# The up-projection's recombination moved into PSUM banks, and the convolution with it, in a decoder layer on one core

## The chip, the core and the metric

The kernel runs on one core of a Trainium2 chip. TensorE multiplies matrices: it loads a 128x128 weight tile and streams up to 512 columns past it into a bank of PSUM (eight banks of 128 partitions x 512 float32 values). VectorE (DVE in the profile) and ScalarE (ACT) read and write PSUM and the on-chip memory SBUF; GpSimd (POOL) works on SBUF alone; SyncE (SP) issues most DMAs. Each engine works through its own list of instructions in order, and they wait for each other by semaphores. The metric is the device time of one execution in microseconds.

## The reference

One layer on 1024 tokens of 1024 channels, all float32: norm, two kinds of attention with gates, residual, then the part that the change concerns:

```python
def conv_ffn(xn, w_up, conv_w, conv_b, w_down):
    S = xn.shape[1]
    u = xn @ w_up
    upad = jnp.pad(u, ((0, 0), (CONV_WIDTH - 1, 0), (0, 0)))
    c = conv_b
    for j in range(CONV_WIDTH):
        c = c + upad[:, j:j + S] * conv_w[j]
    gate, val = jnp.split(c, 2, axis=-1)
    return (jax.nn.silu(gate) * val) @ w_down
```

Before it stands `rmsnorm(x, norm_ffn_w)`, after it a residual addition and a final norm.

## The kernel before

Everything is kept with channels on partitions and tokens along the row. To keep float32 accuracy each matrix product is made of three matmuls: high half of the weights with high and low half of the activations, low half of the weights with the high half (`product`, lines 828 to 837; a product over 512 input channels into one bank of 128 output channels x 512 tokens is 4 x 3 = 12 matmuls).

The up-projection (`hidden`, lines 839 to 914) runs over 22 pairs j. A pair is 128 gate channels and the 128 value channels that belong to them. Over the two blocks of output channels, the two halves of the input channels and the two halves of the tokens it is a 2 x 2 x 2 product of blocks, and is computed with the seven products of Strassen's method in Winograd's form instead of eight. The weights' blocks are A11, A12 (gate) and A22 (value), and sums S1 to S4 that GpSimd makes (`sum_pair`, lines 86 to 100); ScalarE rounds each to its high half and VectorE subtracts to get the low half (`split_pair`, lines 102 to 115, with the tiles wh and wl for A11/A12 and for A22, two of each, and sh and sl for the sums, three of each). `next_w` keeps this two pairs ahead in the program's order. The activations' blocks B11, B21, B22 and the sums T1 to T4 are made once before.

The seven products P1 = A11 B11, P2 = A12 B21, P5 = S1 T1, P6 = S2 T2, P7 = S3 T3, P3 = S4 B22, P4 = A22 T4 each take a bank of the pool `psF`, eight banks in turn. `recombine` (lines 389 to 402) puts them together: ScalarE copies P1 to SBUF, and VectorE makes seven additions of 512 columns, each of a bank and an SBUF tile, through u2 = P1 + P6, u3 = u2 + P7 and u4 = u2 + P5:

- c11 = P1 + P2 (gate, first tokens), c12 = u4 + P3 (gate, last tokens),
- c21 = u3 - P4 (value, first tokens), c22 = u3 + P5 (value, last tokens).

`glu` (950 to 960) and `conv` (962 to 973) then do, for gate and value, on 1024 columns in SBUF: multiplication by the norm's factor `rstd` (GpSimd, L965; for gate and value of pair 0 VectorE), bias and last tap (ScalarE, L970), two taps (VectorE, L971 and L972); then ScalarE's silu of the gate (L957), VectorE's product of both (L958), and a store of the pair's result to DRAM by SyncE (L959). For the first pair `rstd` itself is spread over the partitions by TensorE's transposes between products.

The order on each engine is set by a planner: of what is ready by its own estimate, it takes what the program issues first. The value convolution of pair 20 and both of pair 21 are put off into the down-projection (`defer`), which begins on the same banks under another pool (`psD`) once they are free.

Of the kernel before, what the change touches and what calls it, by code (L numbers as in the profile page):

```python
# [12 lines left out]
AF = mybir.ActivationFunctionType  # L13
# [4 lines left out]
P = 128  # L18
D = 1024
T = 1024  # L20
# [22 lines left out]
class Trunk:  # L43
# [206 lines left out]
    def project(self):  # L250
# [6 lines left out]
        with ExitStack() as ctx:  # L257
# [22 lines left out]
            def diffs(k):  # L280
# [6 lines left out]
                tt(b, b2, b, ALU.subtract)  # L287
# [101 lines left out]
    def recombine(self, ps, us, tp, o):  # L389
# [12 lines left out]
        tt(c21, u3, ps["P4"], ALU.subtract)  # L402
# [400 lines left out]
    def operands(self, xt, xtp, xw, k):  # L803
# [22 lines left out]
        tt(t4, t2, b21, ALU.subtract)  # L826
# [12 lines left out]
    def hidden(self, pair):  # L839
        nc, tc = self.nc, self.tc  # L840
        with ExitStack() as ctx:
            e = ctx.enter_context
            psF = e(tc.tile_pool(name="psF", bufs=8, space=PSUM, reuse_waits="tile"))
            self.psT = psF
# [6 lines left out]
            ready = {}  # L851
            for j in range(NF):
                w, ps = ready.pop(j) if j else (w0, {})
                if j == 0:
# [9 lines left out]
                    ssq = self.tl(psF, [P, H2], "t")  # L864
# [14 lines left out]
                for name, a, b in (prods[i] for i in ((0, 1, 2, 5, 3, 6, 4) if j == NF - 1 else (0, 1, 2, 5, 3, 4, 6) if j else range(7))):  # L879
                    if name not in ps:  # L880
                        ps[name] = self.tl(psF, [P, H2], "t")
                        self.product(ps[name], w[a], b)
                us = [self.tl(tp, [P, T + 2], "us", bufs=3) for _ in range(2)]
                if j == NF - 1:
                    self.defer.pop(0)(lo)
                    self.xctx2.close()
                    self.uw = None
                    self.open_down()
                    self.deep = True
                    with tc.high_priority(100):  # L890
                        self.ahead(2)
                self.recombine(ps, us, tp, 2)
                if j < NF - 1:
# [6 lines left out]
                    for name, a, b in prods[:2 if j == 0 else 0]:  # L900
                        ps[name] = self.tl(psF, [P, H2], "t")
                        self.product(ps[name], w[a], b)
                if j == 0:
                    for hf in range(2):
                        sp = self.tl(psF, [P, H2], "t")
                        self.spread(sp, rs, hf * 4)
                        nc.scalar.copy(self.rstd[:, hf * H2:(hf + 1) * H2], sp)

                for w in range(2):
                    f = lambda after=None, j=j, w=w, us=us: self.glu(j, w, us[w], tp, after)  # L910
                    if j + w < NF - 1:
                        f()
                    else:
                        self.defer.append(f)
# [296 lines left out]
```

## Time and profile before

| | |
|---|---|
| median of 3 runs | 1356.72 us (1356.71 to 1357.4) |
| the profiled execution | 1356.2 us, span of its instructions 1354.3 us |
| granted TensorE clock, mean | 0.996 |
| the up-projection's products | from about 684 us to 1111 us of the span |

In a timeline, each row is: start in us, duration in us, engine, line, operation, output tile <- input tiles, shape, count, and in brackets the idle time before it and what ended it. Tile names come from the program; every bank of `psF` is called t. In a table of windows, each row is: window, its length, then busy time and instruction count of TensorE, its weight loads, VectorE, ScalarE and GpSimd, granted clock, share of the DMA engines, GB/s. In a list of groups: line, engine, operation, tiles, shape, count, busy us, mean ns of one, idle us before them and what ended it. In a list of waits: who waited for whom, us in total, times, longest. `L837 t<-B_0h,wl` is a product's third matmul on its first block of input channels.

### The profile page before, as it was taken

Reading aid. Unit: us, or ns where it says so; the run is one execution under the profiler, and the core shown is the slowest. Engines: PE = TensorE matmul, PEld = TensorE weight load, DVE = VectorE, ACT = ScalarE, POOL = GpSimd, SP = SyncE. Lnnn points to the kernel's source line nnn. Section 1 sums busy time; section 2 is a strip of 40 time slices with the busy share of each in tenths; the row PEclk is TensorE's granted clock in tenths of the full one; section 3 lists DMA queues with packets and bytes.
Section 4 is the critical chain, followed back from the end, with each engine's and each line's share of the span. In section 5 each row is a group of like instructions: output and inputs, shape, how many; then the busy total and the mean of one; then the engine's idle time right before and its main releaser. Section 6 shows DMA issues by size and latency. Waiting matters only on the chain.

```text
span 1354.3 us, 17160 instructions
## 1 busy us (share of the span) xinstructions
PE 1335.0 (99%) x6304; PEld 1103.6 (81%) x6304; DVE 1009.8 (75%) x1454; ACT 603.9 (45%) x942; POOL 483.1 (36%) x350
## 2 busy tenths in 40 slices
PE   7999999999999999999999999999999999999997
PEld 6888888888887777878888888888888888888886
DVE  8846775388898875355689888888888898986454
ACT  8422232376667664334444334433443345433343
POOL 0436651010102125741455565555555611231011
PEclk9999999999999999999999999999999999999999
DMA  6334443966554235334422222122212248651342
GB/s 255 140 113 164 143 156 114 272 174 175 156 133 144 77 116 219 117 119 136 166 82 88 71 91 94 62 79 93 93 63 83 92 141 311 215 177 64 94 134 85
DMA packets 62470, 179.50 MB, mean 133 GB/s; under 512 B 6833, under 2 KB 15153, under 8 KB 62385
## 3 DMA queue, kind: packets, MB, share of 16 engines
q1 hardware_dynamic: 50928, 160.98, 36.7%
q10 hardware_dynamic: 11456, 17.41, 3.5%
q8 instruction: 50, 0.82, 0.2%
q14 instruction: 36, 0.29, 0.1%
HBM read 129.61 MB, written 48.76 MB: 132 GB/s over the span
## 4 chain that ended last, share of the span: by engine, by line
PE 62%; DVE 17%; POOL 7%; issue 7%; DMA 4%; ACT 3%; POOLq 0%; DVEq 0%; SPq 0%; ACTq 0%
PE t L836 7%; PE t L837 7%; PE t L835 7%; POOL us L965 3%; PE y L996 3%; PE d L996 3%; PE sc L568 3%; PE g L150 2%; PE g L151 2%; DVE c L958 2%; PE g L152 2%; DVE wl L112 2%; DMA gr<-gd 2%; PE sc L151 2%; PE sc L152 2%
## 5 line engine op out<-in xcount | busy, mean ns | idle before, releaser
L970 ACT ACTIVATE c<-us,vecs 128x1024 f32<-128x1024 f32 x44 | 54.8, 1248 | 163.2 <-POOL us L965 160.0
L965 POOL TENSOR_TENSOR us<-us,rstd 128x1024 f32<-128x1024 f32 x42 | 100.7, 2414 | 52.8 <-DVE wl L131 34.3
L110 ACT CAST sh<-sf 128x1024 fp32r<-128x1024 f32 x62 | 64.9, 1051 | 106.2 <-POOL sf L97 61.8
L129 ACT CAST wh<-raw 128x1024 fp32r<-128x1024 f32 (+2 forms) x60 | 60.7, 1012 | 104.8 <-PE sc L151 33.1
L971 DVE SCALAR_TENSOR_TENSOR c<-us,vecs,c 128x1024 f32<-128x1024 f32 x44 | 67.1, 1527 | 51.9 <-ACT c L970 51.9
L131 DVE TENSOR_TENSOR wl<-raw,wh 128x1024 fp32r<-128x1024 f32 (+2 forms) x60 | 75.3, 1256 | 39.1 <-ACT wh L129 29.3
L96 POOL TENSOR_TENSOR sf<-rv 128x512 f32<-128x512 f32 x30 | 42.5, 1417 | 166.7 <-DMA rv<-in_w_up 73.2
L112 DVE TENSOR_TENSOR sl<-sf,sh 128x1024 fp32r<-128x1024 f32 x62 | 88.3, 1426 | 8.2 <-ACT sh L110 8.2
L167 POOL TENSOR_TENSOR rs<-ms,mhalf 128x8 f32<-128x8 f32 (+2 forms) x9 | 14.5, 1614 | 159.1 <-DVE ms L165 148.5
L150 PE MATMUL g<-xh,wh 128*128 128x512 f32 x176 | 70.7, 402 | 0.1
L152 PE MATMUL g<-xh,wl 128*128 128x512 f32 x176 | 70.4, 400 | 0.0
L151 PE MATMUL g<-xl,wh 128*128 128x512 f32 x176 | 70.4, 400 | 0.0
L98 POOL TENSOR_TENSOR sf<-raw,rv 128x512 f32<-128x512 f32 x30 | 41.6, 1386 | 59.9 <-DVE sl L112 59.9
L572 DVE CUSTOM_DVE_ANT_0 L<-sc,bias 128x128 f32<-128x128 f32 (+7 forms) x64 | 47.7, 752 | 17.4 <-PE sc L568 14.1
L551 POOL MEMSET aT<- 128x128 f32 x32 | 6.1, 204 | 152.0 <-PE t L597 101.6
L573 ACT ACTIVATE L<-L,sm 128x128 f32<-128x128 f32 (+7 forms) x64 | 49.6, 778 | 20.7 <-DVE sm L572 18.2
L97 POOL TENSOR_TENSOR sf<-sf,raw 128x512 f32<-128x512 f32 x31 | 58.0, 1870 | 1.6
L972 DVE SCALAR_TENSOR_TENSOR c<-us,vecs,c 128x1024 f32<-128x1024 f32 x44 | 56.2, 1279 | 0.6
L725 POOL TENSOR_TENSOR gr<-gr,rstd 128x1024 f32<-128x1024 f32 x16 | 39.4, 2467 | 41.4 <-DMA gr<-gd 41.2
L112 DVE TENSOR_TENSOR wl<-raw,wh 128x1024 fp32r<-128x1024 f32 (+1 forms) x35 | 52.8, 1508 | 0.1
L151 PE MATMUL sc<-ml,wh 128*128 128x512 f32 x128 | 50.1, 391 | 0.6 <-DVE ml L746 0.6
L568 PE MATMUL sc<-u,u 128*128 128x512 f32 (+2 forms) x192 | 49.8, 359 | 0.1
(444 smaller groups left out, 4351.4 us busy)
## 6 DMA issues: line engine op xcount, KB each, us to landing
u<-qd SPq DMA_DIRECT2D x72, 256.0 KB, 6.1
raw<-in_w_down SPq DMA_DIRECT2D x27, 512.0 KB, 3.7
raw<-in_w_in SPq DMA_DIRECT2D x25, 512.0 KB, 4.4
hr<-hd SPq DMA_DIRECT2D x50, 256.0 KB, 5.3
raw<-in_w_up SPq DMA_DIRECT2D x23, 512.0 KB, 3.6
hd<-c SPq DMA_DIRECT2D x22, 512.0 KB, 2.8
rv<-in_w_up SPq DMA_DIRECT2D x21, 512.0 KB, 3.5
gr<-gd SPq DMA_DIRECT2D x16, 512.0 KB, 3.6
```

The costliest lines, as they stand in the source:

```text
L112: nc.vector.tensor_tensor(lo, src, hi.bitcast(F32), ALU.subtract)
L131: self.lo = (eng or nc.vector).tensor_tensor(wl, raw, wh.bitcast(F32), ALU.subtract)
L150: nc.tensor.matmul(ps, wh[:, kc + o, :], ah, start=first and n == 0, stop=False)
L151: nc.tensor.matmul(ps, wh[:, kc + o, :], al, start=False, stop=False)
L152: nc.tensor.matmul(ps, wl[:, kc + o, :], ah, start=False, stop=last and n == len(kcs) - 1)
L568: nc.tensor.matmul(sc[:, lo + n0:lo + n1], qs, k[c][part][:, n0:n1], start=part == 0, stop=part == 1)
L835: nc.tensor.matmul(ps, ah[:, k, :], bh, start=first and n == 0, stop=False, skip_group_check=skip)
L836: nc.tensor.matmul(ps, ah[:, k, :], bl, start=False, stop=False, skip_group_check=skip)
L837: nc.tensor.matmul(ps, al[:, k, :], bh, start=False, stop=last and n == len(ks) - 1, skip_group_check=skip)
L965: i = (nc.vector if m % NF == 0 else nc.gpsimd).tensor_tensor(us[:, 2:], us[:, 2:], self.rstd, ALU.mult)
L971: nc.vector.scalar_tensor_tensor(c, us[:, 1:T + 1], cw[1], c, ALU.mult, ALU.add)
L996: nc.tensor.matmul(ps, v[:, n, :], x, start=n == i == 0, stop=n == len(js) - 1 and i == 2)
```

## The change

From the second pair on (j >= 1), the seven products go through four banks a, b, c, d instead of seven, and most sums are made by letting further matmuls add to what a bank holds:

- a = A11 B11 (`begin`); ScalarE copies a to b. Then b gets S2 T2 added, which makes u2; ScalarE copies b to c. d = S1 T1, copied by ScalarE to an SBUF tile s5.
- a gets A12 B21 added: c11. c gets S3 T3 added: u3. b gets S4 B22 added.
- VectorE empties a with one multiplication by `rstd` (`scaled`); out of c it adds s5 to make c22, out of b it adds s5 to make c12 (`summed`), and GpSimd multiplies these two halves by `rstd`.
- c then gets A22 T4 added and is emptied by `scaled`: c21. T4 has its sign turned where it is made, here and in the first projection, so that it can be added.
- The order of products is a pair's A11, the previous pair's A22 (`last`, issued by the next pair through `rest`), then S2, S1, A12, S3, S4. In pair 1 S1's product stands ahead, before the norm's transposes; in the last pair A22 follows S4 directly.

The convolution from pair 1 on is made in halves of 512 columns in two banks, psC: ScalarE's first tap writes the bank, VectorE's two taps work in it, ScalarE's silu or VectorE's product takes it out to SBUF. One of the two banks has a tag of its own (s). The value convolution of a pair is issued in the next pair, after A22's product. The convolutions of pair 21, in the down-projection, stay in SBUF at full width, without the multiplication by `rstd`, which is done before.

```diff
@@ -284,7 +284,7 @@
-                tt(b, b2, b, ALU.subtract)
+                tt(b, b, b2, ALU.subtract)
@@ -399,7 +399,7 @@
-        tt(c21, u3, ps["P4"], ALU.subtract)
+        tt(c21, ps["P4"], u3, ALU.add)
@@ -823,7 +823,7 @@
-        tt(t4, t2, b21, ALU.subtract)
+        tt(t4, b21, t2, ALU.subtract)
@@ -840,15 +840,15 @@
         nc, tc = self.nc, self.tc
         with ExitStack() as ctx:
             e = ctx.enter_context
-            psF = e(tc.tile_pool(name="psF", bufs=8, space=PSUM, reuse_waits="tile"))
-            self.psT = psF
+            psF = self.psT = e(tc.tile_pool(name="psF", bufs=7, space=PSUM, reuse_waits="tile"))
+            self.psC = None
             xc2 = e(tc.tile_pool(name="xc2", bufs=1, side="right", reuse_waits="tile"))
             self.uw = e(tc.tile_pool(name="uw", bufs=3, side="right", reuse_waits="tile"))
             prods = (("P1", "A11", "B11"), ("P2", "A12", "B21"), ("P5", "S1", "T1"), ("P7", "S3", "T3"),
                      ("P3", "S4", "B22"), ("P6", "S2", "T2"), ("P4", "A22", "T4"))
             with tc.high_priority(400):
                 w0 = self.split_pair(*pair)
-            ready = {}
+            ready, rest = {}, None
             for j in range(NF):
                 w, ps = ready.pop(j) if j else (w0, {})
                 if j == 0:
@@ -861,7 +861,7 @@
                         self.B["T4", k], self.B["T2", k] = ((hi[:, c], lo[:, c]) for c in (slice(0, H2), slice(H2, T)))
                     self.tctx.close()
                     tp = e(tc.tile_pool(name="tp", bufs=2, side="right", reuse_waits="tile"))
-                    ssq = self.tl(psF, [P, H2], "t")
+                    ssq = self.tl(psF, [P, H2], "s", bufs=1)
                     for n, (name, a, b) in enumerate(prods[:5]):
                         self.product(ps[name], w[a], b, (3,), first=False)
                         if n == 4:
@@ -876,20 +876,25 @@
                                 h = self.tl(self.uw, [P, 2, H2], ("sh", "sl", "rv", "rv", "sh", "sl")[2 * k + hf], F32R, **({"bufs": 2} if k == 1 else {}))
                                 self.hs[hf, k] = self.split(h[:, 0], h[:, 1], r[:, hf * H2:(hf + 1) * H2])
                         lo = self.lo
-                for name, a, b in (prods[i] for i in ((0, 1, 2, 5, 3, 6, 4) if j == NF - 1 else (0, 1, 2, 5, 3, 4, 6) if j else range(7))):
-                    if name not in ps:
-                        ps[name] = self.tl(psF, [P, H2], "t")
-                        self.product(ps[name], w[a], b)
-                us = [self.tl(tp, [P, T + 2], "us", bufs=3) for _ in range(2)]
-                if j == NF - 1:
-                    self.defer.pop(0)(lo)
-                    self.xctx2.close()
-                    self.uw = None
-                    self.open_down()
-                    self.deep = True
-                    with tc.high_priority(100):
-                        self.ahead(2)
-                self.recombine(ps, us, tp, 2)
+                if j == 0:
+                    for name, a, b in prods:
+                        if name not in ps:
+                            ps[name] = self.tl(psF, [P, H2], "t")
+                            self.product(ps[name], w[a], b)
+                    us = [self.tl(tp, [P, T + 2], "us", bufs=3) for _ in range(2)]
+                    self.recombine(ps, us, tp, 2)
+                else:
+                    us, last = self.chain(w, ps or self.begin(psF, w), tp, rest)
+                    rest = last
+                    if j == NF - 1:
+                        self.defer.pop(0)(lo)
+                        self.xctx2.close()
+                        self.uw = None
+                        self.open_down()
+                        self.deep = True
+                        with tc.high_priority(100):
+                            self.ahead(2)
+                        rest()
                 if j < NF - 1:
 
                     w, ps = ready[j + 1] = self.next_w(), {}
@@ -897,21 +902,76 @@
                         raw = [self.tl(self.sfp[0], [P, T], "t42", bufs=1)] + [self.tl(self.sfp[0], [P, T], "sf") for _ in range(2)]
                         for k, r in enumerate(raw):
                             nc.sync.dma_start(r, self.hd[k])
-                    for name, a, b in prods[:2 if j == 0 else 0]:
-                        ps[name] = self.tl(psF, [P, H2], "t")
-                        self.product(ps[name], w[a], b)
                 if j == 0:
+                    ps.update(self.begin(psF, w))
+                    self.product(ps["d"], w["S1"], "T1")
                     for hf in range(2):
-                        sp = self.tl(psF, [P, H2], "t")
+                        sp = self.tl(psF, [P, H2], "s", bufs=1)
                         self.spread(sp, rs, hf * 4)
                         nc.scalar.copy(self.rstd[:, hf * H2:(hf + 1) * H2], sp)
 
-                for w in range(2):
-                    f = lambda after=None, j=j, w=w, us=us: self.glu(j, w, us[w], tp, after)
-                    if j + w < NF - 1:
-                        f()
+                if j:
+                    self.psC = [self.tl(psF, [P, H2], "s", bufs=1), self.tl(psF, [P, H2], "t")]
+                first, second = (lambda after=None, j=j, w=w, us=us: self.glu(j, w, us[w], after, j > 0) for w in range(2))
+                if j == NF - 1:
+                    self.defer += [first, second]
+                else:
+                    first()
+                    if j == NF - 2:
+                        self.defer.append(second)
+                    elif j == 0:
+                        second()
                     else:
-                        self.defer.append(f)
+                        rest = lambda last=last, second=second: (last(), second())
+
+    def begin(self, pool, w):
+
+        ps = {n: self.tl(pool, [P, H2], "t") for n in "adbc"}
+        self.product(ps["a"], w["A11"], "B11", skip=True)
+        self.nc.scalar.copy(ps["b"], ps["a"])
+        return ps
+
+    def chain(self, w, ps, tp, rest):
+
+        nc = self.nc
+        tt = nc.vector.tensor_tensor
+        a, b, c, d = (ps[n] for n in "abcd")
+        us = [None, None]
+
+        def half(r, hf):
+            if us[r] is None:
+                us[r] = self.tl(tp, [P, T + 2], "us", bufs=3)
+            return us[r][:, 2 + hf * H2:2 + hf * H2 + H2], self.rstd[:, hf * H2:(hf + 1) * H2]
+
+        def scaled(r, hf, p):
+            u, rs = half(r, hf)
+            tt(u, p, rs, ALU.mult)
+
+        def summed(r, hf, p):
+            u, rs = half(r, hf)
+            tt(u, p, s5, ALU.add)
+            nc.gpsimd.tensor_tensor(u, u, rs, ALU.mult)
+
+        if rest:
+            rest()
+        self.product(b, w["S2"], "T2", first=False, skip=True)
+        nc.scalar.copy(c, b)
+        if rest:
+            self.product(d, w["S1"], "T1")
+        s5 = self.tl(tp, [P, H2], "s1", bufs=1)
+        nc.scalar.copy(s5, d)
+        self.product(a, w["A12"], "B21", first=False, skip=True)
+        scaled(0, 0, a)
+        self.product(c, w["S3"], "T3", first=False, skip=True)
+        summed(1, 1, c)
+        self.product(b, w["S4"], "B22", first=False, skip=True)
+        summed(0, 1, b)
+
+        def last():
+            self.product(c, w["A22"], "T4", first=False, skip=True)
+            scaled(1, 0, c)
+
+        return us, last
 
     def open_down(self):
         tc = self.tc
@@ -947,30 +1007,39 @@
         tt(b21, b22, b21, ALU.subtract)
         self.B["T4", k] = self.parts_h(b21)
 
-    def glu(self, j, w, us, tp, after):
-
-        nc = self.nc
-        c = self.conv(j + w * NF, us, tp, after)
+    def glu(self, j, w, us, after, scaled):
+
+        nc = self.nc
         if w == 0:
-            self.c0 = c
+            self.c0 = self.tl(self.cpl, [P, T], "c")
+        for c, a, b in self.conv(j + w * NF, us, after, scaled):
+            g = self.c0[:, a:b]
+            if w == 0:
+                nc.scalar.activation(g, c, AF.Silu)
+            else:
+                nc.vector.tensor_tensor(g, g, c, ALU.mult)
+        if w == 0:
             return
-        nc.scalar.activation(self.c0, self.c0, AF.Silu)
-        nc.vector.tensor_tensor(self.c0, self.c0, c, ALU.mult)
         store = lambda c0=self.c0: nc.sync.dma_start(self.hd[j], c0)
         self.late.append(store) if after is not None else store()
 
-    def conv(self, m, us, tp, after=None):
+    def conv(self, m, us, after, scaled):
         nc = self.nc
         nc.gpsimd.memset(us[:, 0:2], 0.0)
-        i = (nc.vector if m % NF == 0 else nc.gpsimd).tensor_tensor(us[:, 2:], us[:, 2:], self.rstd, ALU.mult)
-        if after is not None:
-            self.tc.add_manual_dep(i.ins, after.ins.name, mybir.DependencyInfo(mybir.DependencyClass.Sync, mybir.DependencyReason.DATA), reason="later")
-        c = self.tl(self.cpl, [P, T], "c")
+        if not scaled:
+            (nc.vector if m % NF == 0 else nc.gpsimd).tensor_tensor(us[:, 2:], us[:, 2:], self.rstd, ALU.mult)
         cw = [self.vecs[:, C_CW + 3 * m + k:C_CW + 3 * m + k + 1] for k in range(3)]
-        nc.scalar.activation(c, us[:, 2:], AF.Identity, bias=self.vecs[:, C_CB + m:C_CB + m + 1], scale=cw[2])
-        nc.vector.scalar_tensor_tensor(c, us[:, 1:T + 1], cw[1], c, ALU.mult, ALU.add)
-        nc.vector.scalar_tensor_tensor(c, us[:, 0:T], cw[0], c, ALU.mult, ALU.add)
-        return c
+        for a, b in ((0, H2), (H2, T)) if self.psC else ((0, T),):
+            if self.psC:
+                c = self.psC[a // H2]
+            else:
+                c = self.c0 if m < NF else self.tl(self.cpl, [P, T], "c")
+            i = nc.scalar.activation(c, us[:, 2 + a:2 + b], AF.Identity, bias=self.vecs[:, C_CB + m:C_CB + m + 1], scale=cw[2])
+            if after is not None:
+                self.tc.add_manual_dep(i.ins, after.ins.name, mybir.DependencyInfo(mybir.DependencyClass.Sync, mybir.DependencyReason.DATA), reason="later")
+            nc.vector.scalar_tensor_tensor(c, us[:, 1 + a:1 + b], cw[1], c, ALU.mult, ALU.add)
+            nc.vector.scalar_tensor_tensor(c, us[:, a:b], cw[0], c, ALU.mult, ALU.add)
+            yield c, a, b
 
     def down(self):
 
@@ -982,6 +1051,7 @@
             self.uw = e(tc.tile_pool(name="uwd", bufs=2, side="right", reuse_waits="tile"))
             self.hpb = e(tc.tile_pool(name="hpb", bufs=HPB, side="right", reuse_waits="tile"))
             self.sfp = self.cpl, "c"
+            self.psC = None
             self.B = {}
             tt = nc.vector.tensor_tensor
             bank = lambda n: self.tl(psD, [P, H2], "dy"[n])
```

## The prediction

> **What bounds the kernel now.** I read the page's busy table and its chain first, then the up-projection in stretches, then who waited for whom, then one period of each engine's timeline.
>
> ```profile
> span 1354.3 us, 17160 instructions
> PE 1335.0 (99%) x6304; PEld 1103.6 (81%) x6304; DVE 1009.8 (75%) x1454; ACT 603.9 (45%) x942; POOL 483.1 (36%) x350
> ```
>
> TensorE is nearly always busy, so only holes in its stream can be won. Windows of the up-projection (us, then busy time and instructions of each engine):
>
> ```profile
> 706.26:726.22 19.96, 19.96 (x94) 16.60 (x92) 19.67 (x19) 10.79 (x12) 12.20 (x9) 1.00 0.26 80
> 726.22:821.42 95.20, 95.20 (x422) 78.85 (x420) 81.07 (x79) 36.46 (x39) 53.83 (x40) 1.00 0.25 83
> 821.42:1072.61 251.19, 250.94 (x1093) 204.05 (x1092) 215.45 (x209) 97.22 (x104) 141.82 (x105) 1.00 0.25 82
> 1072.61:1111.07 38.46, 38.38 (x169) 31.45 (x168) 34.76 (x40) 14.85 (x19) 13.35 (x11) 1.00 0.29 92
> ```
>
> A pair is 7 products of 12 matmuls, 84 weight loads. The second row is 420 of them, five pairs (2 to 6): 95.20/420 = 0.2267 us each, 2.72 us a product, 19.04 a pair, and nothing is lost. The third is 13 pairs: 251.19 against 1092 x 0.2267 = 247.5, so 3.65 us lost. The fourth is the last two: 38.46 against 38.08, 0.38 lost. **All that the up-projection after its first pair can give back is 4.0 us, 0.30% of the run.** What is lost, and to whom:
>
> ```profile
> PEld t L837 <- DVE wl L112: 5.7, 14, 0.5
> ACT c L970 <- POOL us L965: 152.9, 39, 8.8
> DVE c L971 <- ACT c L970: 49.7, 22, 2.8
> ```
>
> In 14 pairs the third matmul waits for the low half of the next pair's A11/A12, a VectorE subtraction. VectorE is late because of a loop, here in one pair:
>
> ```profile
> 899.24 2.31 DVE L958 TENSOR_TENSOR c<-c,c 128x1024 f32<-128x1024 f32 x1
> 901.47 0.68 DVE L397 TENSOR_TENSOR u<-t,s 128x512 f32<-128x512 f32 x1
> ...
> 905.31 0.69 DVE L401 TENSOR_TENSOR us<-t,u 128x512 f32<-128x512 f32 x1
> ...
> 910.31 1.72 DVE L971 SCALAR_TENSOR_TENSOR c<-us,vecs,c 128x1024 f32<-128x1024 f32 x1 [2.58 <-ACT c L970]
> ...
> 916.27 0.69 DVE L396 TENSOR_TENSOR us<-t,s 128x512 f32<-128x512 f32 x1
> 916.87 1.75 DVE L112 TENSOR_TENSOR wl<-raw,wh 128x1024 fp32r<-128x1024 f32 x1
> ```
>
> Recombination ends in L401, GpSimd scales the result (L965), ScalarE starts the convolution (L970), VectorE goes on with it, recombines the next pair, makes the weights. Third row: 215.45/13 = 16.6 us of VectorE work a pair, and the 2.6 us wait; that is a loop of 19.3 us (251.19/13), just longer than TensorE's 19.04. Eight banks let TensorE run ahead until pair 7, when the lead is used up.
>
> **What the change does to a pair.** Rows by shape, from pairs 2 to 19 (18 pairs):
>
> ```profile
> L971 DVE SCALAR_TENSOR_TENSOR c<-us,vecs,c 128x1024 f32<-128x1024 f32 x36 | 54.7, 1519 | 46.8 <-ACT c L970 46.8
> L972 DVE SCALAR_TENSOR_TENSOR c<-us,vecs,c 128x1024 f32<-128x1024 f32 x36 | 46.0, 1279 | 0.6
> L958 DVE TENSOR_TENSOR c<-c,c 128x1024 f32<-128x1024 f32 x18 | 39.8, 2212 | 0.0
> L112 DVE TENSOR_TENSOR wl<-raw,wh 128x1024 fp32r<-128x1024 f32 x18 | 32.8, 1825 | 0.0
> L396 DVE TENSOR_TENSOR us<-t,s 128x512 f32<-128x512 f32 x18 | 12.3, 684 | 0.0
> L112 DVE TENSOR_TENSOR wl<-rv,wh 128x512 fp32r<-128x512 f32 x18 | 12.2, 679 | 0.0
> L110 ACT CAST wh<-raw 128x1024 fp32r<-128x1024 f32 x18 | 18.6, 1034 | 0.0
> L970 ACT ACTIVATE c<-us,vecs 128x1024 f32<-128x1024 f32 x36 | 44.9, 1248 | 136.5 <-POOL us L965 136.5
> L957 ACT ACTIVATE c<-c 128x1024 f32<-128x1024 f32 x18 | 19.1, 1063 | 24.3 <-DVE c L972 24.3
> L395 ACT COPY s<-t 128x512 f32<-128x512 f32 x18 | 10.2, 565 | 2.3 <-PE t L837 2.3
> L965 POOL TENSOR_TENSOR us<-us,rstd 128x1024 f32<-128x1024 f32 x36 | 86.7, 2426 | 6.7 <-DVE us L401 4.6
> L99 POOL TENSOR_TENSOR sf<-raw,sf 128x512 f32<-128x512 f32 x18 | 24.3, 1348 | 0.0
> ```
>
> TensorE: the same 84 matmuls; sums that VectorE made before are now accumulations in a bank, so the term is nothing, and what could cost are waits. VectorE loses 7 additions of 0.68 (4.8), four full convolution steps 2 x (1.519 + 1.279) = 5.6, one product of 2.21: 12.6 us. It gains 2 scalings and 2 sums out of banks (4 x 0.68), 8 half convolution steps and 2 half products. No VectorE instruction of the trace writes a bank. From below a half step costs half of L972, 0.64, from above half of the longest L971:
>
> ```profile
> L971 DVE SCALAR_TENSOR_TENSOR c<-us,vecs,c x44: 1272/1502/2309, 718.1 to 1152.3; 128x1024 f32<-128x1024 f32 x44
> ```
>
> that is 1.15. I take 0.68, the 512-wide row with one operand in a bank (L396), as the nearest. Then 9.5 us are added, a net -3.1: 16.6 becomes 13.5. GpSimd: two scalings of 2.43 become two half ones at 1.35 (L99): -2.2. ScalarE: L970 and L957 in halves, about the same (L395's 0.57 to half of L970's, 0.62, each), and two more copies, +1.1, on 7.5: no bound. Loads and the store are as many as before; the second half of a pair's weights is read one product later, so its buffer and the next load behind it on SP's queue come 2.7 us later, with a whole pair of lead.
>
> ```profile
> 726.22 0.39 PE L835 MATMUL t<-B_0h,wh 128*128 128x512 f32 x1
> ```
>
> **The new waits**, on a clock that starts with a pair's first product (A11, to bank a); the order is a, the previous pair's A22, S2, S1, A12, S3, S4. Each has everything later on TensorE behind it.
> - S2 waits for ScalarE's copy a to b (0.57). Cover: one product, 2.72. Copy c from b: two products. Neither shows if ScalarE is free, slack 2.72 - 0.57 - 0.16 (a matmul's 0.39 less its 0.23 spacing) = 2.0 us.
> - A22 waits until VectorE has added out of bank c. Cover: S4 and the next A11, 5.4 us; in the last pair S4 alone.
> - A11/A12's buffer comes free after the fifth product instead of the second. Cast 1.03 and subtraction 1.83 must fit into S3 and S4 and two matmuls, 5.9 us; slack about 3. Above that the old stall is back.
> - GpSimd's scaling now stands ahead of only one half of each convolution, and the pair's gate can start on its first half after A12. The old loop is cut: what remains of it, 13.5 of VectorE plus the 2.6 wait, is 16.1, three below TensorE's 19.04.
>
> So the 4.0 us go. **What it costs at the ends.** The eight banks that let VectorE lag are gone, and in the first two pairs it does lag:
>
> ```profile
> 711.70 1.03 PE L173 MATMUL t<-ident,rs 128*128 128x128 f32 x8
> 712.49 0.48 PE L835 MATMUL t<-T_0h,sh 128*128 128x512 f32 x1
> ```
>
> ```profile
> 715.56 2.36 DVE L965 TENSOR_TENSOR us<-us,rstd 128x1024 f32<-128x1024 f32 x2
> 718.10 4.29 DVE L971 SCALAR_TENSOR_TENSOR c<-us,vecs,c 128x1024 f32<-128x1024 f32 x2 [0.18 <-ACT c L970]
> ...
> 725.84 0.68 DVE L397 TENSOR_TENSOR u<-t,s 128x512 f32<-128x512 f32 x1
> 726.44 1.72 DVE L958 TENSOR_TENSOR c<-c,c 128x1024 f32<-128x1024 f32 x1
> 728.08 0.68 DVE L398 TENSOR_TENSOR u<-t,u 128x512 f32<-128x512 f32 x1
> ```
>
> Pair 1's S3 ends at about 720.7 (706.26 + 5 products + 0.8 of the norm's transposes, 711.70 to 712.49); its A22 is wanted two products later, at 726.1. VectorE is with pair 0's convolution, still full width, until 725.84: less 1.7 for L396 and the weights that no longer stand ahead, plus 1.5 to 1.8 for the weights, now made in between, and 0.6 for the first scaling, some 726.3. The sum out of bank c then ends at 727.0, or behind L958 at 728.6: 0.9 to 2.5 us late, 0 if the order puts it earlier. I take 1.5. In the last pair the cover is 2.72 and the sum needs 0.16 + 0.68: 0 to 1.0 for one instruction in front, I take 0.3.
>
> The sum: -4.0 + 1.5 + 0.3 = **-2.2 us**. The profiled execution took 1356.2 us (its span of 1354.3 and 1.9 around it), 0.5 below the median of the three runs, 1356.72; the gain is set against the median: **1354.5 us**.
>
> A hole in TensorE's stream can cost more than itself. After 16 one-column matmuls and a wait the trace has:
>
> ```profile
> 699.81:703.03 3.22, 3.22 (x9) 2.11 (x7) 3.22 (x4) 2.62 (x4) 0.10 (x1) 0.50 0.00 0
> 696.59:699.81 3.22, 2.93 (x20) 2.45 (x19) 3.22 (x3) 1.75 (x2) 0.87 (x2) 0.97 0.00 0
> ```
>
> Some 3.2 us of thin work (second row) were followed by 3.2 us at half clock (first row, 0.50), which cost about 1.6. [...]
>
> **Rivals.**
> 1. The start takes the whole gain: 2.5 us late plus 1.6 of half clock against 4.0. For it: VectorE busy 19.67 of 19.96 in pair 1's first row above. Against: TensorE has other products it could run. About 1357, from 1355 to 1360.
> 2. **Slower: the seed copy comes late in every pair.** ScalarE works in order; if the gate's second half (waiting for GpSimd) stands ahead of the copy to b, S2 waits for GpSimd. The sum out of b ends near 0.9, GpSimd with two weight sums ahead (2 x 1.35) and its own 1.35 near 5.0, activation 0.62 and copy 0.57 near 6.2; S2 is wanted at 5.44. 0.75 x 20 = 15 us: 1369.5. It decides from 2.0 us of lateness on; 0.11 us a pair cancels the gain. For it: GpSimd held ScalarE up to 8.8 us in one wait. Against: the scaling now takes half as long.
> 3. Convolution in a bank at 1.15 a step: VectorE 13.5 + 8 x 0.47 = 17.3, plus the wait of 2.6 = 19.9, 0.85 over TensorE: 20 x 0.85 - 2.2 = +15, 1371. Against: L396, which reads a bank, takes no longer than L112's 512-wide row, all in SBUF.
> 4. The change doesn't do it: the weights, with their buffer free three products later, are as late as now. Nothing won, 1.8 paid: 1358.5.
>
> **How the numbers follow.** A measurement of this kernel tells 0.2%, 2.7 us, from no change; the line is 1354.0. Forecast 0.58, its own range 1352 to 1356: 0.33 below the line, 0.25 within. Rival 1: 0.14, 0.10 within and 0.04 slower. Rival 2: 0.16 slower. Rival 3: 0.07 slower. Rival 4: 0.05, 0.02 within, 0.03 slower. Faster 0.33, same 0.37, slower 0.30. Low end 1351.8: all of the 4.0 and some of a later hole, with no cost at the ends. High end 1364 takes in rival 1, rival 4 and half of rival 2, and leaves 0.17 out in all.
>
> **What would show it.** Right: pairs of 19.04 us throughout, no wait of a weight load for wl, VectorE about 13.5 us a pair, one hole of 1 to 3 us at the second pair's start ahead of A22's product. Half convolution steps near 0.68. Wrong: TensorE waiting in every pair, for a ScalarE copy (rival 2), for the sum out of c, or for wl (rival 4); steps over 1 us (rival 3); half clock near 728 (rival 1).

## The result, and the profile after

The changed kernel takes 1369.85 us (median of 5 runs, 1369.18 to 1370.7), the kernel before beside it 1356.71: a ratio of 1.0098, 95% interval 1.0083 to 1.0113. That is 13 us slower, where 2 us faster was forecast, and above the range's 1364. Further down, one of the twelve executions of `seed_first` ran at a granted clock of 0.556 and took 2243.37 us; the ratios compare executions at 0.992 to 0.998 and leave it out.

The page of the changed kernel, busy time by engine:

```profile
span 1368.2 us, 17201 instructions
PE 1340.6 (98%) x6304; PEld 1104.1 (81%) x6304; DVE 980.6 (72%) x1491; ACT 639.4 (47%) x1044; POOL 446.0 (33%) x350
```

The same matmuls, VectorE relieved as intended, ScalarE still under half busy: by shares nothing is wrong. The windows of the up-projection tell where the time went (window, length, busy time and instructions of TensorE, its loads, VectorE, ScalarE, GpSimd, granted clock, DMA share, GB/s):

```profile
706.36:737.66 31.30, 25.50 (x105) 19.39 (x103) 27.98 (x27) 14.57 (x19) 18.87 (x13) 0.95 0.24 84
737.66:1108.43 370.77, 367.56 (x1596) 298.21 (x1596) 289.09 (x345) 175.76 (x250) 167.82 (x149) 1.00 0.24 82
757.17:776.68 19.51, 19.34 (x85) 15.70 (x85) 15.16 (x19) 9.18 (x14) 9.37 (x8) 1.00 0.24 81
```

The first row is pair 1, from its A11 to pair 2's S2: 8 products, 96 x 0.2267 = 21.8 us, and 0.8 of transposes. It took 31.3, so **8.7 us are lost at the start**. The second row is 19 pairs: 370.77/19 = 19.51 us each, against 19.04 of matmuls. **That is 0.47 lost in every pair, 9.0 us in all.** The third row is one of them. Before, 4.0 us were lost in all these pairs and nothing in pair 1, so these make 8.7 + 9.0 - 4.0 = 13.7 us, against 13.9 between the two spans and 13.1 between the medians.

Who waited for whom in the up-projection (total us, times, longest):

```profile
ACT c L1018 <- DVE t L1041: 33.2, 19, 1.8
ACT t L1037 <- POOL us L953: 18.4, 20, 2.9
PEld t L835 <- ACT t L931: 12.1, 20, 0.8
PEld t L835 <- DVE us L952: 3.7, 1, 3.7
PEld t L835 <- ACT t L958: 2.4, 1, 2.4
```

No wait for wl is left: the old loss is gone. In its place TensorE waits 20 times for L931, the seed copy a to b, and at the start once for L958, the copy b to c, and once for L952, the sum out of c. The chain in one pair, from the sum out of b to S2, with VectorE's weight subtraction L112 beside it (TensorE's other rows and one ScalarE cast are left out):

```profile
751.60 0.69 DVE L952 TENSOR_TENSOR us<-t,s 128x512 f32<-128x512 f32 x1 [1.05 <-PE t L837]
752.37 1.09 POOL L953 TENSOR_TENSOR us<-us,rstd 128x512 f32<-128x512 f32 x1 [1.31 <-DVE us L952]
752.51 2.03 DVE L112 TENSOR_TENSOR sl<-sf,sh 128x1024 fp32r<-128x1024 f32 x1 [0.22 <-ACT sh L110]
753.49 0.78 ACT L1037 ACTIVATE t<-us,vecs 128x512 f32<-128x512 f32 x1 [1.01 <-POOL us L953]
754.46 0.74 DVE L1040 SCALAR_TENSOR_TENSOR t<-us,vecs,t 128x512 f32<-128x512 f32 x1
755.24 0.76 DVE L1041 SCALAR_TENSOR_TENSOR t<-us,vecs,t 128x512 f32<-128x512 f32 x1
755.48 0.39 PE L837 MATMUL t<-B_3h,wl 128*128 128x512 f32 x1
756.03 0.60 ACT L1018 ACTIVATE c<-t 128x512 f32<-128x512 f32 x1 [1.75 <-DVE t L1041]
756.52 0.59 ACT L931 COPY t<-t 128x512 f32<-128x512 f32 x1
...
757.17 0.50 PE L835 MATMUL t<-T_0h,sh 128*128 128x512 f32 x1 [0.17 <-ACT t L931]
```

Read it upwards. S2 (757.17) waits for L931. L931's own input, the A11 product, was complete after the matmul of 755.48, but the copy stands behind the silu of the gate's second half (L1018), and that waits for two taps, an activation, GpSimd's scaling and the sum. The copy needs none of these; it only has them ahead of it in one engine's queue. (L112, ahead of the first tap on VectorE, adds 0.2 us: the activation ends at 754.27, the tap starts at 754.46.) From the start of the sum to the end of the copy it is 5.5 us, and TensorE has 24 matmuls (A11 and the last A22, 5.44 us) for that time.

At the start, ScalarE and VectorE:

```profile
717.27 2.37 ACT L1037 ACTIVATE c<-us,vecs 128x1024 f32<-128x1024 f32 x2
719.55 1.03 ACT L110 CAST wh<-raw 128x1024 fp32r<-128x1024 f32 x1
720.48 0.57 ACT L958 COPY t<-t 128x512 f32<-128x512 f32 x1
```

```profile
719.77 4.51 DVE L1040 SCALAR_TENSOR_TENSOR c<-us,vecs,c 128x1024 f32<-128x1024 f32 x2
724.21 2.31 DVE L112 TENSOR_TENSOR wl<-raw,wh 128x1024 fp32r<-128x1024 f32 x1
726.44 2.47 DVE L1041 SCALAR_TENSOR_TENSOR c<-us,vecs,c 128x1024 f32<-128x1024 f32 x2
728.83 0.68 DVE L948 TENSOR_TENSOR us<-t,rstd 128x512 f32<-128x512 f32 x1
729.43 0.67 DVE L952 TENSOR_TENSOR us<-t,s 128x512 f32<-128x512 f32 x1
```

Pair 0's convolution, still at full width, stands ahead of pair 1's copy b to c (wanted at 718.8) and ahead of its sum out of c (wanted at 726.4); a weight cast (L110) stands there too in the one queue, a weight subtraction (L112) in the other. From one matmul's start to the next it is 2.3 and 3.7 us there, 2.1 and 3.5 more than the spacing, and after the second hole TensorE ran 3.3 us at half clock (granted 0.52).

### The profile page after: what moved, and what is told of

Read it like the earlier page. It is cut to its first block, busy times and chain, and to the rows that moved or that the text cites. A ratio compares the mean times of both kernels' runs of the same rounds, so it can differ in the third digit from the quotient of the medians.

```text
span 1368.2 us, 17201 instructions
## 1 busy us (share of the span) xinstructions
PE 1340.6 (98%) x6304; PEld 1104.1 (81%) x6304; DVE 980.6 (72%) x1491; ACT 639.4 (47%) x1044; POOL 446.0 (33%) x350
## 4 chain that ended last, share of the span: by engine, by line
PE 68%; DVE 15%; ACT 6%; POOL 5%; DMA 3%; issue 3%; POOLq 0%; SPq 0%; ACTq 0%; DVEq 0%
PE t L835 9%; PE t L836 9%; PE t L837 8%; PE y L1066 3%; PE d L1066 3%; DVE sl L112 3%; DVE wl L112 3%; PE sc L568 3%; PE g L150 2%; PE g L151 2%; PE g L152 2%; DMA gr<-gd 2%; PE sc L151 2%; PE sc L152 2%; PE sc L150 2%
## 5 line engine op out<-in xcount | busy, mean ns | idle before, releaser
L112 DVE TENSOR_TENSOR sl<-sf,sh 128x1024 fp32r<-128x1024 f32 x62 | 102.8, 1660 | 37.2 <-ACT sh L110 37.2
L110 ACT CAST sh<-sf 128x1024 fp32r<-128x1024 f32 x62 | 65.0, 1051 | 97.5 <-PE t L836 87.1
L99 POOL TENSOR_TENSOR sf<-raw,sf 128x512 f32<-128x512 f32 x31 | 61.5, 1984 | 0.2
L112 DVE TENSOR_TENSOR wl<-raw,wh 128x1024 fp32r<-128x1024 f32 (+1 forms) x35 | 58.9, 1683 | 3.0 <-ACT wh L110 2.9
L953 POOL TENSOR_TENSOR us<-us,rstd 128x512 f32<-128x512 f32 x42 | 48.0, 1145 | 39.4 <-DVE us L952 37.5
L572 DVE CUSTOM_DVE_ANT_0 L<-sc,bias 128x128 f32<-128x128 f32 (+7 forms) x64 | 47.7, 752 | 17.0 <-PE sc L568 13.7
L110 ACT CAST wh<-raw 128x1024 fp32r<-128x1024 f32 (+1 forms) x35 | 35.1, 1003 | 36.8 <-PE t L836 20.1
L152 PE MATMUL sc<-mh,wl 128*128 128x512 f32 x128 | 49.9, 390 | 0.0
L150 PE MATMUL sc<-mh,wh 128*128 128x512 f32 x128 | 49.8, 389 | 0.0
```

What stands on the lines that cost most here:

```text
L99: tt(sb[:, 1], g[:, 1], sa[:, 1], ALU.subtract)
L110: nc.scalar.copy(hi, src)
L112: nc.vector.tensor_tensor(lo, src, hi.bitcast(F32), ALU.subtract)
L150: nc.tensor.matmul(ps, wh[:, kc + o, :], ah, start=first and n == 0, stop=False)
L152: nc.tensor.matmul(ps, wl[:, kc + o, :], ah, start=False, stop=last and n == len(kcs) - 1)
```

## The experiments

In each diff `add_manual_dep(x, y, NoSync)` puts x behind y in their engine's order and adds no wait of its own. Line numbers move by a few lines from kernel to kernel. "Loss" is the time by which successive matmul starts in a trace lie further apart than 0.227 us, added up; ratios are against the kernel before, run beside each.

| run | median us | ratio, 95% interval | loss 704 to 765 us | loss 765 to 1105 us |
|---|---|---|---|---|
| before | 1356.71 | | 0.2 | 4.1 |
| the change | 1369.85 | 1.0098 (1.0083 to 1.0113) | 9.5 | 8.3 |
| order | 1372.16 | 1.0123 (1.0106 to 1.0139) | 12.7 | 8.0 |
| silu | 1360.38 | 1.0042 (1.0027 to 1.0057) | 9.7 | 0.0 |
| prio | 1373.72 | 1.0139 (1.0124 to 1.0154) | 13.9 | 8.1 |
| from2 | 1369.19 | 1.0104 (1.0089 to 1.0119) | 10.5 | 8.0 |
| late_conv0 | 1367.05 | 1.0094 (1.0080 to 1.0108) | 9.1 | 8.1 |
| copy_first | 1359.98 | 1.0039 (1.0025 to 1.0053) | 10.0 | 0.0 |
| late_conv0_silu | 1358.79 | 1.0028 (1.0017 to 1.0040) | 8.6 | 0.0 |
| conv_sbuf | 1384.73 | 1.0220 (1.0204 to 1.0235) | 9.2 | 23.8 |
| seed_first | 1352.62 | 0.9981 (0.9972 to 0.9990) | 2.3 | 0.0 |
| seed_first_sbuf | 1356.71 | 1.0012 (1.0003 to 1.0021) | 5.9 | 0.5 |

**order.** The previous pair's A22 behind all of the next A11, where the planner had woven the two together.

```diff
+        self.a11 = self.mm
...
         if rest:
-            rest()
+            with self.tc.issue_after(self.a11.ins):
+                rest()
```

> The changed kernel, with A22's twelve matmuls put behind the last of the next pair's A11 (in the changed kernel seven stand ahead of A11 and five behind, so the copy of bank a to b has 5 x 0.227 = 1.1 us of cover instead of 2.7). Theory (short cover): S2 no longer waits, pairs of 19.04 us instead of 19.51, 20 x 0.47 = 9.4 us less, 1360.5 us. Rival (the weights of A11/A12, which have one buffer, come late and are why A22 was split): TensorE then waits for wl ahead of A11, pairs stay near 19.5, time within 2 us of the changed kernel's 1369.9.

The pairs did not change. ScalarE in one pair:

```profile
875.44 0.60 ACT L1020 ACTIVATE c<-t 128x512 f32<-128x512 f32 x1 [1.75 <-DVE t L1043]
875.94 0.59 ACT L932 COPY t<-t 128x512 f32<-128x512 f32 x1
```

Now A11 ends a whole product before S2, and the copy still comes right behind the silu. Its data is early; its place in the queue is late. The theory that the copy had too little cover falls. The rival falls as well, for TensorE doesn't wait for wl there. The start lost 3.2 us more than in the change, which neither had foreseen.

**silu.** One line: the silu of the gate's second half behind the next pair's seed copy.

```diff
+            self.tc.add_manual_dep(self.silu.ins, self.seed.ins.name, mybir.DependencyInfo(mybir.DependencyClass.NoSync, mybir.DependencyReason.DATA), reason="seed first")
```

> The changed kernel, with ScalarE's silu of the gate's second half (0.60 us) put behind the next pair's copy of bank a to b; TensorE's order untouched, 5 matmuls of cover. Theory (the copy queues behind the silu): the copy starts when bank a is done, 0.6 us earlier, the 0.33 us hole ahead of S2 closes, pairs of 19.04 to 19.1 us, 8 to 9.4 us less, 1360.5 to 1362. Rival (the copy is late for its own data, or ScalarE is short of time): hole and time as in the changed kernel, 1370.

Windows of this run:

```profile
704.00:765.00 61.00, 54.46 (x232) 43.29 (x232) 52.30 (x55) 29.15 (x39) 31.69 (x24) 0.97 0.25 86
765.00:1105.00 340.00, 340.00 (x1501) 281.53 (x1501) 275.48 (x320) 164.38 (x235) 143.42 (x139) 1.00 0.24 81
```

In the second row TensorE has no idle time at all: 340/1501 = 0.2265 us a matmul. The theory held, to 0.2 us. Swapping two entries of one queue took away the 8.3 us of loss in this stretch; by the two ratios it brought 7.6 us (9.5 between the medians, which were taken beside different runs of the kernel before). The work on ScalarE is the same. The first row shows the start untouched, so it is another loss.

**prio** and **from2** were aimed at the start: pair 1's chain planned ahead of pair 0's convolution, and pair 1 left in the old form, so that the chain begins with pair 2.

```diff
-                    us, last = self.chain(w, ps or self.begin(psF, w), tp, rest)
+                    with tc.high_priority(150) if j == 1 else nullcontext():
+                        us, last = self.chain(w, ps or self.begin(psF, w), tp, rest)
```

> The changed kernel, with the first chained pair (j = 1) planned ahead of pair 0's convolution on ScalarE, VectorE and GpSimd. Theory (what costs 8.8 us at the start is the queue's order: the copy of b to c behind pair 0's two activations, the sum out of c behind its taps): the two holes of 2.1 and 3.5 us and the half clock after them go, 6 to 7 us less, 1363 to 1364. Rival (VectorE has too much work there, in any order): the holes move to the next pair's products, within 1.5 us of 1369.9.

```diff
-                if j == 0:
+                if j < 2:
...
-                if j:
+                if j > 1:
                     self.psC = [self.tl(psF, [P, H2], "s", bufs=1), self.tl(psF, [P, H2], "t")]
```

> The changed kernel, with pair 1 still recombined as before (seven banks, convolution at full width), the chain from pair 2 on. Theory (it is pair 0's convolution together with the norm's start that the chain meets): the start loses less than 3 us instead of 8.8, pairs from 3 on unchanged at 19.51: 1363 to 1365. Rival (the loss belongs to the change of form itself, wherever it is): the holes stand one pair later with the same 8.8 us, 1369 to 1370.

Neither got rid of it, and in both the time is nearest to the rival's. In prio the higher priority also held up the norm's transposes, and TensorE then waited for two seed copies (4.2 us the longer wait). In from2 the loss is one hole, one pair later:

```profile
741.52 1.06 ACT L1022 ACTIVATE c<-c 128x1024 f32<-128x1024 f32 x1 [2.83 <-DVE c L1045]
742.49 0.58 ACT L962 COPY t<-t 128x512 f32<-128x512 f32 x1
```

```profile
743.12 0.79 PE L835 MATMUL t<-T_0h,sh 128*128 128x512 f32 x1 [7.07 <-ACT t L962]
```

Here the copy b to c stands behind the full-width silu of the pair that is in the old form. So the loss at the start does not belong to the norm or to pair 1. As far as this run shows, it belongs to **the first chained pair, which finds a full-width convolution ahead of its copies**.

**late_conv0**, **late_conv0_silu** and **copy_first.** Pair 0's convolution issued behind pair 1's chain, its first taps behind pair 1's sum out of c, and a fourth buffer for rows, without and with the edit of silu. In copy_first, silu's kernel, pair 0's two convolution activations alone are moved behind pair 1's copy b to c.

```diff
-                    first()
+                    if j == 0:
+                        conv0 = first, second
+                    else:
+                        first()
...
                     us, last = self.chain(w, ps or self.begin(psF, w), tp, rest)
+                    if j == 1:
+                        self.psC = None
+                        conv0[0](), conv0[1]()
...
+            if not scaled:
+                self.tc.add_manual_dep(i.ins, self.sumc.ins.name, mybir.DependencyInfo(mybir.DependencyClass.NoSync, mybir.DependencyReason.DATA), reason="order")
```

> The same start as in 'late_conv0_silu', with the silu left where the change has it. Theory (two separate losses that add): the start's 9 to 10 us go, pairs stay at 19.51 us, 1359.5 to 1361.5 us. Rival (the start's loss comes from the same wait on the silu as the pairs', or from the clock alone): less than 3 us go, 1367 us or more.

> Three edits to the changed kernel: the gate's second-half silu is put behind the next pair's seed copy on ScalarE (as in the run 'silu'); pair 0's convolution is emitted behind pair 1's products, and its first taps on VectorE are put behind pair 1's sum out of bank c; a fourth buffer for the recombined rows, so that this sum doesn't wait for pair 0's convolution. Theory: the start loses its time (9.7 us of spacing over 0.227 us in 'silu') to two in-order queues, ScalarE's and VectorE's, in which pair 0's full-width convolution stands ahead of pair 1's copy b to c and sum out of c. Then the start's loss falls below 2 us, pairs stay at 19.04 us, and the time is 1360.4 - 8 to 10 = 1350.5 to 1352.5 us, under the kernel before. Rival: the work only moves, and pair 2 then waits as pair 1 did (as in 'from2'): the loss at the start stays at 8 us or more, 1358 to 1361 us.

```diff
-        nc.scalar.copy(c, b)
+        self.cb = nc.scalar.copy(c, b)
+        if not rest:
+            for x in self.act0:
+                self.tc.add_manual_dep(x.ins, self.cb.ins.name, mybir.DependencyInfo(mybir.DependencyClass.NoSync, mybir.DependencyReason.DATA), reason="order")
```

> 'silu' with one more edit: pair 0's two full-width convolution activations are put behind pair 1's copy b to c on ScalarE; VectorE's order stays. Theory: the first hole at the start (2.1 us over the spacing, and the 2.6 us of half clock behind it) belongs to ScalarE's queue alone and goes, the holes ahead of A22 and of pair 2's S2 (VectorE's queue) stay: 1355 to 1358 us. Rival: VectorE sets the start throughout, and the time that is won at the first hole is lost at the second: 1359.5 to 1361 us.

In all three the rivals held. The holes that were aimed at went, and the time came back at the next wait. In copy_first the hole ahead of S3 is gone and the one ahead of A22 has grown from 2.1 to 5.9 us (sum out of c, VectorE). In late_conv0_silu both are gone and S2 of pair 2 waits 4.4 us. ScalarE there:

```profile
729.01 0.78 ACT L1048 ACTIVATE t<-us,vecs 128x512 f32<-128x512 f32 x1 [4.86 <-POOL us L1039]
729.81 1.28 ACT L1029 ACT_TABLE_LOAD   x1
731.10 1.06 ACT L1029 ACTIVATE c<-c 128x1024 f32<-128x1024 f32 x1
732.07 0.58 ACT L938 COPY t<-t 128x512 f32<-128x512 f32 x1
```

It is the pairs' mechanism once more. The seed copy L938 (A11 of pair 2 complete at 728.0) stands behind an activation that waits for GpSimd, a table load and pair 0's silu. The two losses are separate, though: with the same start, the silu's place is worth 8.3 us (1367.05 to 1358.79).

**conv_sbuf.** The convolution's part of the change undone: the two lines that give it banks are left out, so that it runs at full width in SBUF; seeds, chain and P5 stay.

```diff
-                if j:
-                    self.psC = [self.tl(psF, [P, H2], "s", bufs=1), self.tl(psF, [P, H2], "t")]
```

> The convolution's part of the change undone: it stays in SBUF at full width, while seeds, chain and P5 stay as changed. In this kernel's ScalarE order the seed copy stands ahead of the gate's silu (one full-width activation behind all taps) and behind the first full-width convolution activation alone. Theory (the pairs lose their 0.47 us to the copy's place behind the second-half silu): pairs at 19.04 to 19.1 us, the start's loss stays at 8 to 12 us, 1359 to 1363 us. Rival (VectorE cannot keep up with a chain whose convolution is at full width, so that the sums and copies come late): pairs at 19.4 us or more, 1366 us or more.

This was a miss, and in the unexpected direction: TensorE waits 1.6 us a pair for the seed copy in place of 0.6. The time lies where the rival put it (1366 us or more), though the rival's cause, a VectorE that cannot keep up, is refuted below by seed_first_sbuf. ScalarE and GpSimd in one pair:

```profile
797.22 1.24 ACT L1035 ACTIVATE c<-us,vecs 128x1024 f32<-128x1024 f32 x1 [3.92 <-POOL us L951]
798.37 0.58 ACT L929 COPY t<-t 128x512 f32<-128x512 f32 x1
```

```profile
794.13 3.06 POOL L951 TENSOR_TENSOR us<-us,rstd 128x512 f32<-128x512 f32 x2
```

The seed copy L929 is ahead of the silu here, as I had read from the order, but behind the activation that starts the convolution. That one waits for the gate's scaling, the second of the two, and GpSimd does both late, one after the other, behind a weight sum that ends at 794.1 (its row, 792.81, is in the last section). I had looked for the silu ahead of the copy; what counts is **anything ahead of it that waits for the pair's last products**.

**seed_first** tests that statement. To late_conv0_silu it adds that, in every pair, the second half's activation and silu of the gate stand behind the next seed copy, in pair 2 pair 0's silu and table load too. The two halves swap their banks, since the held-back half must not hold one of the banks in turn.

```diff
-        if rest and self.psC:
-            self.tc.add_manual_dep(self.silu.ins, self.seed.ins.name, mybir.DependencyInfo(mybir.DependencyClass.NoSync, mybir.DependencyReason.DATA), reason="seed first")
+        if rest:
+            for x in self.behind:
+                if x is not self.act0:
+                    self.tc.add_manual_dep(x.ins, self.seed.ins.name, mybir.DependencyInfo(mybir.DependencyClass.NoSync, mybir.DependencyReason.DATA), reason="order")
+            self.behind = []
```

> 'late_conv0_silu' with one more edit: in the ScalarE queue the seed copy of the next pair stands ahead of every activation that waits for the pair's last products (the second half's convolution activation and silu of the gate row) and, for pair 2, ahead of pair 0's silu and the table load; the two halves swap their banks, so that the held-back half has the bank of its own. Theory: the 4.4 us hole at 728.28 in 'late_conv0_silu' and the half clock behind it (8.6 us of spacing over 0.227 us in all) belong to that copy's place alone; the loss at the start falls to 0 to 2 us and the pairs stay at 19.04 us: 1350.5 to 1352.5 us, below the kernel before. Rival: VectorE's backlog of two convolutions surfaces at the next wait, pair 2's sum out of c ahead of A22, with 2 to 4 us and half clock behind it: 1354 to 1357 us.

```profile
704.00:765.00 61.00, 59.88 (x266) 48.39 (x265) 56.62 (x61) 31.71 (x42) 37.79 (x30) 1.00 0.29 95
765.00:1105.00 340.00, 340.00 (x1502) 281.53 (x1501) 278.21 (x324) 166.98 (x235) 137.76 (x134) 1.00 0.24 81
```

```profile
726.60 0.57 ACT L940 COPY t<-t 128x512 f32<-128x512 f32 x1 [1.82 <-PE t L838]
```

The copy now waits for TensorE's product (the bracket of its row), as it should, and TensorE waits for it only once, for 0.4 us. 1352.62 against 1355.34 us for the kernel before, 0.9981 (0.9972 to 0.9990). **This version beats both kernels**, the one before by 2.7 us, which is 0.2%, and, by the two ratios, the change as it was made by 16. The change's idea was worth about what it was taken for; the order in the queues cost six times as much. What the fourth buffer for rows did alone, within these 16 us, was not measured.

**seed_first_sbuf.** The same with the convolution at full width in SBUF.

> 'seed_first' with the convolution back in SBUF at full width (as in 'conv_sbuf'). Theory: 'conv_sbuf' lost 1.55 us a pair because its seed copy stands behind the full-width convolution activation, which waits for both scalings on GpSimd; with the copy ahead of it the width and place of the convolution no longer matter, pairs take 19.04 to 19.1 us and the time is within 2 us of 'seed_first'. Rival: at full width VectorE or GpSimd cannot keep the chain's dates (sums out of c and b behind 1.28 us taps, scalings at 2 us): pairs at 19.3 us or more, at least 5 us above 'seed_first'.

```profile
765.00:1105.00 340.00, 339.87 (x1500) 281.16 (x1499) 280.25 (x236) 158.78 (x184) 166.71 (x139) 1.00 0.24 81
```

The theory holds for the pairs: conv_sbuf's 23.8 us of loss fell to 0.5, with the same convolution. The time lies between theory and rival, 4.1 us above seed_first: the start loses 5.9 us in place of 2.3. One hole of 2.8 us at 743.4 and the half clock behind it (granted 0.51) make 4.3 of the 5.9; there pair 3's A11 waits for the low half of its weights, which VectorE makes late. So by these two kernels the convolution in PSUM is worth 0.5 us in all the pairs and some 4 us at the start.

## Why the prediction was wrong, step by step

- **What can be won: right.** 4.0 us lost in the pairs before, none in silu and seed_first (340.00 of 340.00 us busy).
- **VectorE a pair: mis-sized, without effect.** 13.5 us were forecast, 15.16 measured. A half step in a bank took 0.748 in place of 0.68, which is 8 x 0.068 = 0.54. The rest is in the weights' low halves:

```profile
L112 DVE TENSOR_TENSOR sl<-sf,sh 128x1024 fp32r<-128x1024 f32 x34 | 53.6, 1575 | 27.1 <-ACT sh L110 27.1
L112 DVE TENSOR_TENSOR wl<-raw,wh 128x1024 fp32r<-128x1024 f32 x17 | 36.3, 2134 | 2.5 <-ACT wh L110 2.5
```

  In the same stretch of the kernel before:

```profile
L112 DVE TENSOR_TENSOR sl<-sf,sh 128x1024 fp32r<-128x1024 f32 x34 | 41.2, 1213 | 0.0
L112 DVE TENSOR_TENSOR wl<-raw,wh 128x1024 fp32r<-128x1024 f32 x17 | 30.5, 1796 | 0.0
```

  Two of the first and one of the second a pair make 2 x 0.36 + 0.34 = 1.06, together 1.6 of the 1.66. VectorE still had 4 us to spare a pair.
- **"S2 waits for ScalarE's copy ... Neither shows if ScalarE is free, slack ... 2.0 us": this step failed.** ScalarE was idle more than half the time, but its queue wasn't free: what stood ahead of the copy was itself waiting. The slack was reckoned from durations; it had to be reckoned from the date at which the instruction ahead is released. The 2.0 us came out as -0.47 in each pair. The cover was also shorter than the one product that was assumed, for the planner left only five matmuls, 1.1 us, between A11 and S2; but order gave the whole product back, and the pairs stayed as they were. In the rows of order and conv_sbuf the copy starts 0.1 us before the end of the instruction ahead of it, which had itself waited 1.75 and 3.92 us; in silu, with the copy put ahead, the pairs lost nothing.
- **Rival 2 named the mechanism** and got 0.16 of the chances. Its size was built on other terms: it let GpSimd end near 5.0 behind two weight sums. In the trace GpSimd was idle and began 0.1 us after the sum; what filled the time were two taps and the silu, which the rival left out. Its 0.75 x 20 = 15 us came out as 0.47 x 19 = 9.0.
- **The start: 1.5 us forecast, 8.7 measured.** Only one of three waits was priced, the sum out of c, at 0.9 to 2.5 us late; it was 3.5. The copy b to c, put down as covered by two products, was late by 2.1 behind pair 0's activations and a weight cast. Both have one main cause, pair 0's full-width convolution ahead in two queues, and whatever is moved there brings up the next wait; from2, copy_first and late_conv0_silu each show another one.
- **Half clock**: rival 1 had 1.6 us for it at the start, the sum of the forecast nothing, and it was there (granted 0.52 behind the 3.7 us hole; behind the 2.3 us hole the clock stayed at 1.00).
- **The end: 0.3 forecast, none seen.** In silu TensorE is busy for all of the last 20 us:

```profile
1095.00:1115.00 20.00, 20.00 (x90) 16.56 (x89) 12.73 (x18) 7.42 (x13) 2.99 (x4) 1.00 0.22 71
```
- **Rivals 3 and 4 fell**: half steps far below 1.15 us, and no wait for wl.

With the queue set right, the sum of the prediction is nearly met: -2.2 forecast, -2.7 (-3.8 to -1.4) measured in seed_first. By its trace that is -4.1 in the pairs and +2.1 at the start. The first is the gain that was forecast; that the second is near the +1.5 is luck. It holds no wait of A22 for the sum out of c: the largest part is one hole of 1.3 us ahead of the norm's transposes, which wait for GpSimd.

## What to carry to other kernels

Where a change makes TensorE wait for a short instruction on a half-idle engine, ask what is queued ahead of it and for what that waits; an in-order queue passes on the wait of its slowest entry (here 1.75 us, ahead of a copy of 0.59), and a busy share of 47% says nothing of it. Let copies that feed the bounding engine stand ahead of everything that hangs on a long chain, and look at the first round separately, where old and new forms meet. A hole that has moved rather than gone can be a sign that the queue, not the instruction, is late.

## What the runs showed of the hardware

**Holes and the granted clock.** Length alone does not decide in these traces whether the clock falls behind a hole, and what else does is not shown. Two holes of the change, each from the last matmul's start to the next one's, and a stretch behind each:

```profile
718.79:721.10 2.31, 0.39 (x2) 0.00 (x0) 2.31 (x2) 2.29 (x4) 2.25 (x2) 1.00 0.00 0
721.10:724.40 3.30, 3.30 (x14) 2.74 (x15) 3.30 (x3) 1.25 (x1) 3.30 (x2) 1.00 0.02 5
726.45:730.16 3.71, 0.39 (x2) 0.00 (x0) 3.71 (x6) 1.61 (x2) 0.20 (x2) 1.00 0.46 141
730.96:734.24 3.28, 3.28 (x10) 2.50 (x8) 2.98 (x4) 0.40 (x1) 3.27 (x2) 0.52 0.39 160
```

The same in silu:

```profile
717.94:720.26 2.32, 0.39 (x3) 0.01 (x1) 2.32 (x2) 2.30 (x4) 2.25 (x2) 1.00 0.00 0
721.55:724.53 2.98, 2.98 (x8) 2.32 (x7) 2.98 (x2) 0.00 (x0) 2.98 (x2) 0.50 0.00 0
734.68:736.82 2.14, 0.39 (x3) 0.01 (x1) 2.14 (x4) 1.14 (x3) 0.00 (x0) 1.00 0.37 149
736.82:740.00 3.18, 3.18 (x14) 2.65 (x15) 2.26 (x5) 2.49 (x5) 0.00 (x0) 1.00 0.14 43
```

The hole of 2.31 us in the change left the clock at 1.00; the one of 2.32 us in silu was followed by 0.50. Behind holes of 2.79 us (seed_first_sbuf), 3.08 (prio), 4.42 (late_conv0_silu) and 7.46 (from2) it was 0.50 or 0.51, in stretches of 3.15 to 5.60 us. In conv_sbuf the clock stayed at 1.00 behind a hole of 3.2 us (734.43 to 737.65):

```profile
736.32:739.73 3.41, 2.08 (x9) 1.73 (x10) 2.54 (x3) 1.83 (x3) 0.00 (x0) 1.00 0.45 154
```

**Where instructions of VectorE and GpSimd overlap in these rows, the later one took longer.** In conv_sbuf, just ahead of the two scalings of the row shown there (794.13, 3.06 us):

```profile
792.81 1.30 POOL L99 TENSOR_TENSOR sf<-raw,sf 128x512 f32<-128x512 f32 x1
```

```profile
793.34 1.86 DVE L112 TENSOR_TENSOR sl<-sf,sh 128x1024 fp32r<-128x1024 f32 x1 [0.22 <-ACT sh L110]
```

VectorE's L112, 1.21 us on the mean in the stretch of before, starts while L99 runs, ends 1.1 us after L99 and takes 1.86; the two scalings, the first of which starts while L112 runs, end 2.0 us after it and take 3.06 together. In the change's pair above the scaling came first (752.37, 1.09 us), and L112 was the longer (752.51, 2.03 us); it ended 1.1 us after the scaling. What makes the later one longer is not shown.
